# Output projections in pairs of column blocks with seven block products, in a two-layer decoder trunk

## The chip, the core and the metric

The kernel runs on one core of a Trainium2 chip. The core has a matrix engine (PE in the profile, with its weight loads listed as PEld), a vector engine (DVE), a scalar engine (ACT), a general engine (POOL) and SyncE (SP), which here only issues DMAs. Operands lie in SBUF, products are accumulated in eight PSUM banks of 128 x 512 float32. The metric is the device time of one launch in microseconds.

## What is computed

Two pre-norm layers on 256 tokens with 2048 columns, all in float32:

```
for layer in (0, 1):
    xn  = rms_norm(h, norm_mix[layer])
    mix = swa_mlstm_mixer(xn) if layer == 0 else forgetting_attention_mixer(xn)
          # each ends in:  concat(heads) @ w_out        (256 x 2048) @ (2048 x 2048)
    h   = h + mix
    h   = h + swiglu(rms_norm(h, norm_ffn[layer]))      # w_gate, w_up: 2048 x 5632, w_down: 5632 x 2048
out = rms_norm(h, norm_final)
```

The layer 0 mixer has sixteen heads of sliding-window attention (columns 0 to 1023 of its output) and four mLSTM heads (columns 1024 to 2047, 256 each). The layer 1 mixer has sixteen attention heads of 128 columns. The change concerns the product `concat(heads) @ w_out` of both layers.

## The kernel before

**Products.** A float32 product is made from three faster ones: each operand is split into a high part (rounded, a cast on ACT) and a low part (the rest, a subtraction on DVE), and hi x hi, lo x hi and hi x lo are summed in PSUM. Activations are kept split and transposed, in `xh`/`xl` (the normed stream) and `mh`/`ml` (the mixer's output, later the hidden values of the feed-forward part). Each has 16 k tiles of 128 rows by 256 tokens; two neighbouring k tiles are a pair, 0 to 7, and the tokens are two halves t of 128. Weights come in chunks of two k tiles by 512 columns (512 KB): `load_raw` (L101) issues the DMA on SP's queue, `split_chunk` (L156) casts on ACT (L159) and subtracts on DVE (L160). A chunk feeds 12 matmuls of 128 x 512.

**Seven products.** `pair_group` (L373) treats two column blocks at once and walks the eight pairs of k in a given order. A pair marked 0 is plain: two chunks, 24 matmuls. A pair marked 1 is mixed: its 2 x 2 x 2 block product (k tile by token half by column block) is done with 7 block products instead of 8, 21 matmuls. This needs sums of the two weight chunks `ra` and `rb` (tile `t4`, four DVE instructions, L404 to L407), the splits of them (`ht`, `lt`), the high and low parts of the last row of `rb` (`hu`, `lu`) and sums of the four activation blocks (`sums_of`, L222). Three of the seven products go into the plain accumulators, four into banks of their own:

```
three(prods[0], xa[:, t0], la[:, t0], hg[:, 0, :], lg[:, 0, :], first, last)
three(plain[0][0], xb[:, t0], lb[:, t0], hg[:, 1, :], lg[:, 1, :], False, False)
three(plain[1][0], sh[:, 3, :], sl[:, 3, :], hu[:, 1, :], lu[:, 1, :], False, False)
three(prods[1], sh[:, 0, :], sl[:, 0, :], ht[0], lt[0], first, last)
three(prods[2], sh[:, 2, :], sl[:, 2, :], ht[1], lt[1], first, last)
three(prods[3], sh[:, 1, :], sl[:, 1, :], ht[2], lt[2], first, last)
three(plain[0][1], xb[:, t1], lb[:, t1], ht[3], lt[3], False, False)
```

At the end of a group one ACT copy and four DVE additions (L430 to L434) make `c` from the four banks, and `c` is added to the result. Before the change the feed-forward part alone uses `pair_group`; gate and up have three mixed pairs of eight.

**PSUM.** Two pools of four banks: `pa` (tag `acc`) and `pm` (tag `pm`). `bank(par, name)` (L370) picks the pool: a group's four plain accumulators come from one pool and its four product banks from the other, alternating. Attention, mLSTM and all transposes use `pm`.

**SBUF.** `close_layer` (L548) opens the pool `fp` for output projection and feed-forward part together. The mixer's own pools (`ev` with `mp` in it for layer 0, `od` for layer 1) are closed by then in the program's text, so `fp` may be laid where they were. In `fp` are the weight chunks of mixed pairs (`raw`, four slots, `load_raw(..., fp)`), `t4`, `ht`, `lt`, `c`, and the activation sums `sx` and `sd`. Plain chunks use `wr` (four raw slots) and `wp` (six slots each of `hi` and `lo`), which are open all the time; `hg` and `hu` of a mixed pair use `wp` too.

**Order.** Each engine runs a fixed list of instructions. A planner makes it before the run: it walks through the program with its own estimate of durations and gives each engine the first instruction in program order whose operands and buffers it takes to be ready. So later work can be placed between instructions of earlier work.

**The output projection before.** `out_proj` (L353) takes column blocks two by two, n0 = 0 and 2 (called first and second half here). For both blocks it runs k tiles 0 to 11 (six pairs) with `gemm` (L173), then for one block after the other the last four k tiles (pairs 6 and 7), the residual addition `add_out` (L267), `split_scaled` (L233: transposes into `pt`, scaled splits into `xh`/`xl`, and `sums_of` for three pairs that the feed-forward part mixes) and `square_sum`. All four accumulators are in `pa`; `pt` is in `pm`.

**What comes ahead of it.** In layer 0: the V projections (L807) and, for each of four heads, `mlstm` (L768): `pc` (L770), its copy `ce` on DVE (L771), two products `pom` (L777, L779), a normalisation over DVE, ACT and POOL on `hv`, and the transposes `ptv` (L802) that become one pair of `mh`/`ml`: head 0 gives pair 4, head 3 pair 7. In layer 1: `attention` on four heads at a time; the last call gives pairs 6 and 7 (`po`, L341 and L342).

Of the kernel before, what the change touches and what calls it, by code (L numbers as in the profile page):

```python
# [7 lines left out]
F32 = mybir.dt.float32  # L8
# [4 lines left out]
ALU = mybir.AluOpType  # L13
# [4 lines left out]
P = 128  # L18
D = 2048
S = 256  # L20
NT = S // P
KT = D // P
FF = 5632
NB = 512
# [13 lines left out]
    6: ((0, 0), (0, 1), (1, 2), (0, 3), (0, 4), (0, 5)),  # L38
    8: ((0, 0), (0, 1), (0, 3), (1, 2), (0, 4), (1, 5), (0, 6), (0, 7)),
}  # L40
MID = 6
MID_DOWN = 5
RAWS = 4
# [3 lines left out]
def mixed_of(order):  # L47
    return [p for w, p in order if w]
# [5 lines left out]
def trunk(  # L54
# [20 lines left out]
    nc = tc.nc  # L75
# [89 lines left out]
    def new_acc():  # L165
        return [pa.tile([P, NB], F32, tag="acc", name="acc") for _ in range(NT)]
# [6 lines left out]
    def gemm(acc, lhs, w, c0, n, k_from, k_to, k_all, skew=1):  # L173
        k0 = k_from
        while k0 < k_to:
            last = k_to == k_all and k0 + skew * CK >= k_all
            chunks = [load_chunk(w, kc, c0, n) for kc in range(k0, k_all if last else k0 + CK, CK)]
            order = [(i, t) for i in range(len(chunks) * CK) for t in range(NT)]
            if last:
                order.sort(key=lambda it: it[1])  # L180
            for i, t in order:
                k = k0 + i
                hi, lo = (c[:, i % CK, 0:n] for c in chunks[i // CK])
                ah, al = lhs(k)
                ts = slice(t * P, (t + 1) * P)
                o = acc[t][:, 0:n]
                nc.tensor.matmul(o, ah[:, ts], hi, start=(k == 0), stop=False)  # L187
                nc.tensor.matmul(o, ah[:, ts], lo, start=False, stop=False)  # L188
                nc.tensor.matmul(o, al[:, ts], hi, start=False, stop=(k == k_all - 1))  # L189
            k0 += len(chunks) * CK  # L190
# [14 lines left out]
    def square_sum(key, n):  # L205
        if n == 0:
            sums[key] = sm.tile([P, NT, 4], F32, tag="ss", name="ss")
        for t in range(NT):
            junk = sm.tile([P, NB], BF16, tag="junk", name="junk", bufs=1)
            nc.scalar.activation(  # L210
                junk, h[:, t, n * NB : (n + 1) * NB], AF.Square, accum_out=sums[key][:, t, n : n + 1]
            )
# [17 lines left out]
        nc.vector.tensor_tensor(out=s[:, 3, :], in0=full[:, 1, 0, :], in1=s[:, 1, :], op=ALU.subtract)  # L230
        split_plain(sh, sl, s)

    def split_scaled(idx, n, extra=None):  # L233
        for half in range(2):
            pt = pm.tile([P, 2, NT, P], F32, tag="pm", name="pt")
            for i in range(2):
                k = 4 * n + 2 * half + i
                for t in range(NT):
                    nc.tensor.transpose(pt[:, i, t, :], h[:, t, k * P : (k + 1) * P], ident)  # L239
            for i in range(2):  # L240
                k = 4 * n + 2 * half + i
                src = pt[:, i, :, :].rearrange("p t q -> p (t q)")
                g = gT[:, idx * KT + k : idx * KT + k + 1]
                nc.scalar.mul(xh[:, k, :], src, g)
                nc.vector.scalar_tensor_tensor(
                    out=xl[:, k, :], in0=src, scalar=g, in1=xh[:, k, :].bitcast(F32), op0=ALU.mult, op1=ALU.subtract
                )
# [16 lines left out]
    def add_out(acc, n):  # L264
        for t in range(NT):
            o = h[:, t, n * NB : (n + 1) * NB]
            nc.vector.tensor_tensor(out=o, in0=acc[t], in1=o, op=ALU.add)  # L267
# [82 lines left out]
            ks = slice(k_tile + q, k_tile + q + 2)  # L350
            split_plain(mh[:, ks, :], ml[:, ks, :], po)

    def out_proj(w, idx, key, extra):  # L353
        last = KT - 4
        for n0 in (0, 2):
            accs = [new_acc() for _ in range(2)]
            for i in range(2):
                gemm(accs[i], m_of, w, (n0 + i) * NB, NB, 0, last, KT)
            for i in range(2):
                gemm(accs[i], m_of, w, (n0 + i) * NB, NB, last, KT, KT)  # L360
                add_out(accs[i], n0 + i)
                split_scaled(idx, n0 + i, extra)
                square_sum(key, n0 + i)

    def three(o, ah, al, hi, lo, start, stop):
        nc.tensor.matmul(o, ah, hi, start=start, stop=False)  # L366
        nc.tensor.matmul(o, ah, lo, start=False, stop=False)  # L367
        nc.tensor.matmul(o, al, hi, start=False, stop=stop)  # L368

    def bank(par, name):  # L370
        return pm.tile([P, NB], F32, tag="pm", name=name) if par else pa.tile([P, NB], F32, tag="acc", name=name)
# [65 lines left out]
    def ffn(layer, fp, sx, sd, key, idx_next=None, key_next=None, finish=None):  # L437
# [6 lines left out]
        for g0, g1 in zip(PARTS, PARTS[1:]):  # L444
# [82 lines left out]
            for n0 in (0, 2):  # L527
                if end and idx_next is None and n0 == 2:
                    for n in (2, 3):
                        acc = new_acc()  # L530
                        gemm(acc, m_of, wd, n * NB, NB, 0, nk, nk, skew=3 if n == 3 else 1)
                        close(acc, n)
                    continue
                plain, c = pair_group(
                    fp, 1 - n0 // 2, m_of, sums_d, [(wd, n0 * NB), (wd, (n0 + 1) * NB)], order, todo
                )
                todo = []
                if end and idx_next is None:
                    gf = fp.tile([P, D], F32, tag="t4", name="gf", bufs=1)
                    nc.gpsimd.dma_start(gf, norm_final.partition_broadcast(P))  # L540
                for m in range(2):
                    for t in range(NT):
                        o = h[:, t, (n0 + m) * NB : (n0 + m + 1) * NB]
                        nc.vector.tensor_tensor(out=o, in0=c[:, 2 * m + t, :], in1=o, op=ALU.add)
                for m in range(2):
                    close(plain[m], n0 + m)

    def close_layer(layer, w_out, idx, key, **rest):  # L548
        with tc.tile_pool(name=f"fp{layer}", bufs=2) as fp:
            nx = len(mixed_of(ORDER))  # L550
            nd = max(len(mixed_of(o)) for o in DOWN.values())
            sx = [fp.tile([P, nx, 4, P], F32R, name=f"sx{i}", bufs=1) for i in range(2)]
            sd = [fp.tile([P, nd, 4, P], F32R, name=f"sd{i}", bufs=1) for i in range(2)]
            out_proj(w_out, idx, key, (*sx, fp))
            ffn(layer, fp, sx, sd, key, **rest)


# [418 lines left out]
```

## Time and profile before

| | |
|---|---|
| launches | 2135.59, 2135.94, 2136.30 us (median 2135.94) |
| profiled execution | span 2134.3 us from the first to the last instruction |
| VectorE, ScalarE, GpSimd busy | 1665.9, 1235.5, 40.4 us |
| PE's waits of over 1 us in the whole span | 4.1 and 1.1 us for the first loads, 1.2 us for `mh` (L261) |
| HBM read | 404.48 MB, 191 GB/s over the span |

A row of the timeline has start and duration in us, engine, line, operation, output and inputs with their shapes, a count, and in brackets the idle time before it and what ended it. Matmuls are pipelined: a row's duration of 0.39 us overlaps the next, so the distance between starts is what a matmul costs. "SPq" is the queue of DMA issues; when several are merged, the duration reaches from the first to the last.

### The profile page before, as it was taken

How to read it: one execution, taken by the hardware profiler on the slowest of the kernel's cores; microseconds unless marked ns; L12 is line 12 of the kernel's file. 1: busy time of each engine (PE TensorE's matmuls, PEld its weight loads, DVE VectorE, ACT ScalarE, POOL GpSimd, SP SyncE). 2: the span in 40 equal slices, each digit the busy share in tenths (PEclk: the TensorE clock that was granted, in tenths of full speed). 3: DMA queues.
4: the chain of work that ended last, by engine and by line, in shares of the span. 5: the costliest groups of instructions: out<-in, count | busy, mean ns of one | idle time of the engine just before them, and what ended most of it. 6: DMA issues, size and time to landing. Idle time of an engine off the chain costs nothing.

```text
span 2134.3 us, 26801 instructions
## 1 busy us (share of the span) xinstructions
PE 2118.0 (99%) x9772; PEld 1758.6 (82%) x9772; DVE 1665.9 (78%) x2116; ACT 1235.5 (58%) x1564; POOL 40.4 (2%) x61
## 2 busy tenths in 40 slices
PE   8999999999999999999999999999999999999998
PEld 7888888888888888888888888888888888888886
DVE  6665567998899988998745554768998998889984
ACT  6565455665567646666645544556754667556753
POOL 2010000000000000000010000000000000000000
PEclk9999999999999999999999999999999999999999
DMA  8444556666667666776575564655756666656753
GB/s 268 149 151 145 174 183 206 214 210 194 200 205 223 212 206 193 236 210 191 152 236 168 168 178 141 234 185 174 246 187 215 207 207 199 234 188 207 227 198 128
DMA packets 257060, 418.84 MB, mean 196 GB/s; under 512 B 56256, under 2 KB 64544, under 8 KB 256672
## 3 DMA queue, kind: packets, MB, share of 16 engines
q1 hardware_dynamic: 256256, 413.40, 61.1%
q0 software_dynamic: 624, 3.72, 0.5%
q8 instruction: 76, 1.25, 0.2%
q14 instruction: 56, 0.46, 0.1%
q10 hardware_dynamic: 48, 0.02, 0.0%
HBM read 404.48 MB, written 2.11 MB: 191 GB/s over the span
## 4 chain that ended last, share of the span: by engine, by line
PE 98%; ACT 1%; issue 0%; DMA 0%; DVE 0%; POOLq 0%; POOL 0%; DVEq 0%; ACTq 0%
PE acc L367 17%; PE acc L368 17%; PE acc L366 17%; PE acc L187 10%; PE acc L188 10%; PE acc L189 10%; PE prod L368 4%; PE prod L367 4%; PE prod L366 4%; PE pt L239 1%; PE p L290 1%; PE ptm L273 1%; PE po L341 1%; PE pp L333 0%; PE p L283 0%
## 5 line engine op out<-in xcount | busy, mean ns | idle before, releaser
L159 ACT CAST hi<-raw 128x1024 fp32r<-128x1024 f32 (+1 forms) x692 | 705.7, 1033 | 681.2 <-PE acc L368 308.4
L160 DVE TENSOR_TENSOR lo<-raw,hi 128x1024 fp32r<-128x1024 f32 (+1 forms) x692 | 820.4, 1198 | 317.9 <-ACT hi L159 316.3
L367 PE MATMUL acc<-lo,xh 128*128 128x512 f32 x946 | 368.1, 389 | 0.0
L368 PE MATMUL acc<-hi,xl 128*128 128x512 f32 x946 | 366.8, 389 | 0.0
L366 PE MATMUL acc<-hi,xh 128*128 128x512 f32 x946 | 366.4, 389 | 0.0
L187 PE MATMUL acc<-hi,xh 128*128 128x512 f32 (+3 forms) x736 | 276.6, 377 | 0.8 <-ACT hi L159 0.8
L189 PE MATMUL acc<-hi,xl 128*128 128x512 f32 (+3 forms) x736 | 276.6, 376 | 0.0
L188 PE MATMUL acc<-lo,xh 128*128 128x512 f32 (+3 forms) x736 | 276.3, 375 | 0.0
L368 PEld LDWEIGHTS acc<-hi,xl 128*128 128x128 f32 x946 | 177.6, 188 | 36.8
L367 PEld LDWEIGHTS acc<-lo,xh 128*128 128x128 f32 x946 | 177.6, 188 | 36.8
L366 PEld LDWEIGHTS acc<-hi,xh 128*128 128x128 f32 x946 | 177.6, 188 | 36.8
L262 DVE TENSOR_TENSOR lt<-t,ht 128x1024 fp32r<-128x1024 f32 x168 | 199.6, 1216 | 3.6 <-ACT ht L261 3.6
L367 PE MATMUL acc<-lo,mh 128*128 128x512 f32 x514 | 200.3, 390 | 0.0
L366 PE MATMUL acc<-hi,mh 128*128 128x512 f32 x514 | 200.1, 389 | 0.0
L368 PE MATMUL acc<-hi,ml 128*128 128x512 f32 x514 | 198.6, 389 | 0.0
L261 ACT CAST ht<-t 128x1024 fp32r<-128x1024 f32 x168 | 175.0, 1053 | 23.2 <-PE acc L368 13.1
L187 PEld LDWEIGHTS acc<-hi,xh 128*128 128x128 f32 x736 | 138.8, 189 | 24.9 <-ACT hi L159 1.2
L189 PEld LDWEIGHTS acc<-hi,xl 128*128 128x128 f32 x736 | 139.1, 189 | 24.3 <-issue 0.8
L188 PEld LDWEIGHTS acc<-lo,xh 128*128 128x128 f32 x736 | 139.1, 189 | 24.1 <-issue 0.7
L187 PE MATMUL acc<-hi,mh 128*128 128x512 f32 x320 | 125.8, 393 | 1.2 <-ACT mh L261 1.2
L188 PE MATMUL acc<-lo,mh 128*128 128x512 f32 x320 | 125.7, 393 | 0.0
L189 PE MATMUL acc<-hi,ml 128*128 128x512 f32 x320 | 124.0, 390 | 0.0
(306 smaller groups left out, 2768.4 us busy)
## 6 DMA issues: line engine op xcount, KB each, us to landing
raw<-in_w_gate_dram SPq DMA_DIRECT2D x176, 512.0 KB, 4.1
raw<-in_w_up_dram SPq DMA_DIRECT2D x176, 512.0 KB, 4.5
raw<-in_w_down_dram SPq DMA_DIRECT2D x176, 512.0 KB, 4.6
raw<-in_w_in_odd_dram SPq DMA_DIRECT2D x88, 512.0 KB, 3.8
raw<-in_w_in_even_dram SPq DMA_DIRECT2D x64, 512.0 KB, 3.8
raw<-in_w_out_even_dram SPq DMA_DIRECT2D x32, 512.0 KB, 3.5
raw<-in_w_out_odd_dram SPq DMA_DIRECT2D x32, 512.0 KB, 3.9
raw<-in_w_in_odd_dram SPq DMA_DIRECT2D x8, 272.0 KB, 2.9
```

The lines of the kernel that those rows point to most:

```text
L159: latest[0] = nc.scalar.copy(hi[:, :, 0:n], raw[:, :, 0:n])
L160: nc.vector.tensor_tensor(out=lo[:, :, 0:n], in0=raw[:, :, 0:n], in1=hi[:, :, 0:n].bitcast(F32), op=ALU.subtract)
L187: nc.tensor.matmul(o, ah[:, ts], hi, start=(k == 0), stop=False)
L188: nc.tensor.matmul(o, ah[:, ts], lo, start=False, stop=False)
L189: nc.tensor.matmul(o, al[:, ts], hi, start=False, stop=(k == k_all - 1))
L239: nc.tensor.transpose(pt[:, i, t, :], h[:, t, k * P : (k + 1) * P], ident)
L261: nc.scalar.copy(dst_h, src)
L262: nc.vector.tensor_tensor(out=dst_l, in0=src, in1=dst_h.bitcast(F32), op=ALU.subtract)
L273: nc.tensor.transpose(pt[:, i, :], s_, ident)
L366: nc.tensor.matmul(o, ah, hi, start=start, stop=False)
L367: nc.tensor.matmul(o, ah, lo, start=False, stop=False)
L368: nc.tensor.matmul(o, al, hi, start=False, stop=stop)
```

## The change

Both output projections now go through `pair_group`, a half at a time. Pairs 0 and 1 of k are mixed and the other six plain; `OUT` gives the order for each half: the first half begins with plain pairs 2, 3, 4 and takes mixed pairs 0 and 1 at the fourth and the sixth place, the second half takes them at the second and the fifth. The sums of the activations are made at the beginning from `mh + ml`, into `sd` of the pool `fp`. The first half has its accumulators in `pa` and its products in `pm`, the second half the other way round; `split_scaled` takes `pt` from the pool of the half's accumulators. `add_pair` is the addition of `c` to the residual stream, moved out of the feed-forward part.

```diff
+OUT = (
+    ((0, 2), (0, 3), (0, 4), (1, 0), (0, 5), (1, 1), (0, 6), (0, 7)),
+    ((0, 2), (1, 0), (0, 3), (0, 4), (1, 1), (0, 5), (0, 6), (0, 7)),
+)
...
-    def split_scaled(idx, n, extra=None):
+    def split_scaled(idx, n, extra=None, par=1):
         for half in range(2):
-            pt = pm.tile([P, 2, NT, P], F32, tag="pm", name="pt")
+            pt = bank(par, "pt").rearrange("p (i t q) -> p i t q", i=2, t=NT)
...
-    def out_proj(w, idx, key, extra):
-        last = KT - 4
-        for n0 in (0, 2):
-            accs = [new_acc() for _ in range(2)]
-            for i in range(2):
-                gemm(accs[i], m_of, w, (n0 + i) * NB, NB, 0, last, KT)
-            for i in range(2):
-                gemm(accs[i], m_of, w, (n0 + i) * NB, NB, last, KT, KT)
-                add_out(accs[i], n0 + i)
-                split_scaled(idx, n0 + i, extra)
-                square_sum(key, n0 + i)
+    def out_proj(w, idx, key, extra, fp, sd):
+        mixed = mixed_of(OUT[0])
+        for j, pair in enumerate(mixed):
+            full = fp.tile([P, 2, NT, P], F32, tag="tmp", name="full")
+            ks = slice(2 * pair, 2 * pair + 2)
+            nc.vector.tensor_tensor(
+                out=full.rearrange("p i t q -> p i (t q)"),
+                in0=mh[:, ks, :].bitcast(F32),
+                in1=ml[:, ks, :].bitcast(F32),
+                op=ALU.add,
+            )
+            sums_of(fp, sd[0][:, j, :, :], sd[1][:, j, :, :], None, full)
...
+        for half in range(2):
+            n0 = 2 * half
+            plain, c = pair_group(fp, half, m_of, sums_m, [(w, n0 * NB), (w, (n0 + 1) * NB)], OUT[half])
+            add_pair(c, n0)
+            for m in range(2):
+                add_out(plain[m], n0 + m)
+                split_scaled(idx, n0 + m, extra, half)
+                square_sum(key, n0 + m)
...
+    def add_pair(c, n0):
+        for m in range(2):
+            for t in range(NT):
+                o = h[:, t, (n0 + m) * NB : (n0 + m + 1) * NB]
+                nc.vector.tensor_tensor(out=o, in0=c[:, 2 * m + t, :], in1=o, op=ALU.add)
...
-            out_proj(w_out, idx, key, (*sx, fp))
+            out_proj(w_out, idx, key, (*sx, fp), fp, sd)
```

More of the change, by code (lines that the diff above doesn't have):

```diff
@@ L351, in attention, with sums_m @@
             split_plain(mh[:, ks, :], ml[:, ks, :], po)
-    def out_proj(w, idx, key, extra):
-        last = KT - 4
-        for n0 in (0, 2):
-            accs = [new_acc() for _ in range(2)]
-            for i in range(2):
-                gemm(accs[i], m_of, w, (n0 + i) * NB, NB, 0, last, KT)
-            for i in range(2):
-                gemm(accs[i], m_of, w, (n0 + i) * NB, NB, last, KT, KT)
-                add_out(accs[i], n0 + i)
-                split_scaled(idx, n0 + i, extra)
-                square_sum(key, n0 + i)
+    def out_proj(w, idx, key, extra, fp, sd):
[10 more added lines that the diff above has]
+            sums_of(fp, sd[0][:, j, :, :], sd[1][:, j, :, :], None, full)
+        def sums_m(pair):
+            j = mixed.index(pair)
+            return sd[0][:, j, :, :], sd[1][:, j, :, :]
+        for half in range(2):
[11 more added lines that the diff above has]
+                nc.vector.tensor_tensor(out=o, in0=c[:, 2 * m + t, :], in1=o, op=ALU.add)
     def three(o, ah, al, hi, lo, start, stop):
@@ L540, in ffn @@
                     nc.gpsimd.dma_start(gf, norm_final.partition_broadcast(P))
[L541 to L544, printed above, removed]
+                add_pair(c, n0)
                 for m in range(2):
```

## The prediction

> **What bounds the kernel now.** I read the page first: busy shares and the chain that ended last.
>
> ```profile
> PE 2118.0 (99%) x9772; PEld 1758.6 (82%) x9772; DVE 1665.9 (78%) x2116; ACT 1235.5 (58%) x1564; POOL 40.4 (2%) x61
> PE 98%; ACT 1%; issue 0%; DMA 0%; DVE 0%; POOLq 0%; POOL 0%; DVEq 0%; ACTq 0%
> ```
>
> The matrix engine is never without work for long, and the chain is 98% PE: a matmul taken away shortens the kernel, and a hole opened in PE's row lengthens it. So I looked at what PE does around the output projections. First the cost of a matmul and the beginning of the first half in layer 0 (timeline of PE), then how many of its matmuls were done when (stretches of PE restricted to `mh`; hi x hi and lo x hi read `mh`, so 2 of 3 matmuls count, 128 for the 192 of a half).
>
> ```profile
> 253.43 0.39 PE L187 MATMUL acc<-hi,mh 128*128 128x512 f32 x1
> ...
> 254.11 0.39 PE L187 MATMUL acc<-hi,mh 128*128 128x512 f32 x1
> ...
> 253.43:298.19 44.76, 36.03 (x113) 20.85 (x112) 1.36 (x2) 1.74 (x3) 1.00 0.48 166
> 253.43:303.79 50.36, 40.61 (x128) 23.77 (x127) 2.04 (x3) 1.74 (x3) 1.00 0.54 184
> 1338.99:1386.05 47.06, 39.34 (x126) 23.64 (x126) 1.38 (x2) 1.17 (x2) 1.00 0.69 228
> ```
>
> A matmul costs 0.227 us (0.68 for three). In layer 0 the half runs from 253.43 to 303.79, in layer 1 from 1338.99 to 1386.05. At 298.19 some 168 of the 192 were done (113 x 1.5): all but pair 7. That work is the cover under which the mixer's tail runs:
>
> ```profile
> 264.99 0.60 PE L802 MATMUL ptv<-ident,hv 128*128 128x128 f32 x4
> 265.43 0.60 PE L770 MATMUL pc<-ve,kw 128*128 128x257 f32 x2
> 265.86 1.03 PE L777 MATMUL pom<-ve,dt__1258 128*128 128x257 f32 x4
> 266.06 0.42 DVE L771 COPY ce<-pc 128x257 f32<-128x257 f32 x1 [1.51 <-PE pc L770]
> 270.84 0.59 PE L779 MATMUL pom<-ce,qst 128*128 128x257 f32 x2
> 274.77 0.89 DVE L791 SCALAR_TENSOR_TENSOR hv<-hv,st,og 128x256 f32<-128x256 f32 x2 [1.22 <-POOL st L789]
> 279.45 0.60 PE L802 MATMUL ptv<-ident,hv 128*128 128x128 f32 x4
> 296.41 0.60 PE L802 MATMUL ptv<-ident,hv 128*128 128x128 f32 x4
> 298.19 0.50 PE L187 MATMUL acc<-hi,mh 128*128 128x512 f32 x1 [1.18 <-ACT mh L261]
> ```
>
> The mLSTM heads follow each other at 15 to 17 us (the three `ptv` rows). A head's `pc` has its inputs long before, yet starts right behind the transposes of the head ahead (264.99 and 265.43): the buffers of one tag, here `pm`, are handed out in program order. While a head waits, PE does output projection, so that its whole tail of 44.8 us costs PE one hole of 1.18 us.
>
> The last view is SP's queue around the end of each mixer, with SP's waits in the same stretches. The feed-forward part's first mixed pairs are prefetched here: four loads into `raw` of `fp`.
>
> ```profile
> 227.94 68.65 SPq L103 DMA_DIRECT2D raw<-in_w_out_even_dram  x23
> 297.08 0.37 SPq L103 DMA_DIRECT2D raw<-in_w_gate_dram  x1
> 297.50 0.46 SPq L103 DMA_DIRECT2D raw<-in_w_up_dram  x1
> SPq L103 <- PE ptv L802: 0.4, 1, 0.4
> 1360.41 0.38 PE L342 MATMUL po<-t,vtail 128*128 128x128 f32 x2
> 1360.87 0.37 SPq L103 DMA_DIRECT2D raw<-in_w_gate_dram  x1
> 1361.29 0.46 SPq L103 DMA_DIRECT2D raw<-in_w_up_dram  x1
> SPq L103 <- PE po L342: 0.9, 1, 0.9
> ```
>
> In both layers the loads go out right after the mixer's last read of its own tiles (the transposes of `hv`, the last `po`), and SP waits for just these. A load into `fp` has no other tie to `ptv` or `po`: `fp` lies where the mixer's pools lay and opens only when they are done. Before the change nothing in `fp` is needed for 50 us after that.
>
> **The change part by part.** *Removed*: two pairs of eight in each of four halves take 21 matmuls instead of 24: 4 x 2 x 3 = 24 matmuls x 0.227 = 5.4 us, all on the bounding engine; 1.36 us per half.
>
> *Moved, first half*: the mixed pairs' weights, their sums and splits, and the sums of the activations all lie in `fp`, so none can be made before the mixer ends. What PE has ahead of the first mixed pair is three plain pairs, 72 matmuls = 16.3 us, in place of 168. May pair 5 go ahead of the mixed pair? Its `hi` and `lo` come behind `hg` and `hu` in the tag's order, and by the `pc` rows such an order is kept; I take no. The product banks are in `pm` behind `ptv` or `po` in the same way, which comes free at the same time as `fp` and costs nothing more. Loads on SP behind the waiting ones are for pairs which cannot run anyway.
>
> Layer 0: PE does 49 of the 72 by 264.99 (11.56 us less about 0.4 for head 1's L779) and runs dry at about 272.4 (23 x 0.227 behind `pc` and `pom`, which end at 266.7). From there the heads do not wait for PE's fillers: head 2's `hv` is ready at 275.66 (274.77 + 0.89), while its transposes now start at 279.45; then head 3 needs from its first `pom` to `hv` what head 2 needed, 265.86 to 275.66 = 9.8 us, less about 3.5 us by which L779 (270.84, behind fillers) lagged the end of `ce` (266.48). That puts the end of `ptv` at about 283.7, against 297.0 if nothing is shortened; I take 284, since with no filler there is nothing to wait behind. Then the loads. The first pair of `fp` loads landed as follows (the DVE's first use, ended by the DMA):
>
> ```profile
> 304.60 0.69 DVE L404 TENSOR_TENSOR t<-raw 128x512 f32<-128x512 f32 x1 [2.65 <-DMA raw<-in_w_up_dram]
> 1367.80 0.69 DVE L404 TENSOR_TENSOR t<-raw 128x512 f32<-128x512 f32 x1 [3.05 <-DMA raw<-in_w_up_dram]
> raw<-in_w_out_even_dram SPq DMA_DIRECT2D x14, 512.0 KB, 3.5
> ```
>
> That is 7.1 us (from 297.50) and 6.5 us (from 1361.29), with other loads in flight; alone a chunk takes 3.5. Bounds 3.5 and 7.1 us; I take 6, since four chunks go together. So landing at about 290. Then a mixed pair's preparation, from the groups by shape (the ACT row from the page):
>
> ```profile
> L160 DVE TENSOR_TENSOR lo<-raw,hi 128x1024 fp32r<-128x1024 f32 x660 | 797.7, 1221 | 298.0 <-ACT hi L159 296.6
> L159 ACT CAST hi<-raw 128x1024 fp32r<-128x1024 f32 (+1 forms) x692 | 705.7, 1033 | 681.2 <-PE acc L368 308.4
> L262 DVE TENSOR_TENSOR lt<-t,ht 128x1024 fp32r<-128x1024 f32 x168 | 199.6, 1216 | 3.6 <-ACT ht L261 3.6
> L404 DVE TENSOR_TENSOR t<-raw 128x512 f32<-128x512 f32 x84 | 57.5, 685 | 6.8 <-DMA raw<-in_w_up_dram 5.7
> L262 DVE TENSOR_TENSOR lo<-raw,hi 128x512 fp32r<-128x512 f32 x84 | 57.7, 686 | 28.2 <-ACT hi L261 27.7
> L267 DVE TENSOR_TENSOR h<-acc,h 128x512 f32<-128x512 f32 x56 | 37.4, 680 | 3.1 <-PE acc L189 1.8 <-PE acc L368 1.3
> L245 DVE SCALAR_TENSOR_TENSOR xl<-pt,gT,xh 128x256 fp32r<-128x256 f32 x64 | 28.4, 477 | 9.0 <-ACT xh L244 8.7
> ```
>
> On DVE 1.22 + 4 x 0.685 + 0.69 + 2 x 1.22 = 7.1 us, against 4.8 us of PE (21 matmuls) and against 2.4 us of DVE for a plain pair. Of the 186 matmuls 114 are left: 25.8 us on PE, plus 1.0 for the first cast and about 1.2 more because PE catches up with DVE in the first mixed pair: 28 us after landing, 318. Before, the same point was 303.8: **+14 us**.
>
> Layer 1: its half took 47.06 us for 43.5 us of matmuls, so 3.5 us of PE went to attention, about half of it ahead of `po`: 72 matmuls from 1338.99 end at 1357; `po` may move up by half a microsecond, the pool opens at about 1360.2, landing 1366.3, end 1394.3, against 1386.05: **+8 us**.
>
> *Added, hidden*: `full` and the sums of two activation pairs on DVE, at most 2 x (0.69 + 4 x 0.48 + 0.69) = 6.6 us (the 128-column additions priced as the 256-column row), run while the loads are in flight; without that cover they would delay the first mixed pair by as much. The `c` of each half (one ACT copy and four additions of 0.68) and `add_pair` (four of 0.68) come while PE does pairs 6 and 7, 48 matmuls = 10.9 us.
>
> *Second halves*: no gate there. DVE per half: 12 x 1.22 + 2 x 7.1 + 12 x 0.68 + 8 x 0.48 + 2.6 for one pair of feed-forward sums = 43 us, for 186 matmuls (42.2) and 16 transposes (1.8) = 44 us of PE. It just fits, with the first mixed pair at the second place, just behind the boundary where DVE also has `add_out`, the splits and the sums. The product banks there (`acc`) come behind four `pt`. Bounds 0 to 3 us of hole for each, none seen at the feed-forward groups' boundaries, whose first mixed pair is a place later; I take 0.5. So -1.36 + 0.5, twice: **-1.7 us**.
>
> *Clock.* PE's first work after idling runs at half speed. The chain of waits near the start:
>
> ```profile
> 9.47 1.81 PE pt L239 x8
> 11.28 0.43 PE acc L188
> 14.04 0.87 PE pt L239 x8
> 15.37 0.23 PE acc L188
> ```
>
> Eight transposes take 1.81 us and later 0.87, a matmul 0.43 and later 0.23; from 8.25 to 12.14 this cost some 2.1 us. Behind a hole of 7 to 17 us the same may come back, but in those microseconds PE would be waiting for DVE's 7.1 us anyway: 12 matmuls at 0.43 are 5.2 us. I add nothing; the bounds are 0 and 2.1 us for each of two holes. The Trainium skill ("TensorE: Matmul & The Clock Gate", Part 1: The HAM clock gate) states such a gate: after a window of about 3.4 us without activity the array runs at half rate until it has been busy for as long. The duration rows at the start agree in kind, though the granted clock reads 1.00 there. By that page the changed kernel would start cold in both layers, an estimated 1.7 us each if nothing hid it; this would speak for the upper half of the range.
>
> **Sum**: 14 + 8 - 1.7 = +20.3 us on a span of 2134.3. The launches' median is 2135.94, 1.64 above the span, so 2156.2.
>
> **The rivals.**
> *Plain pairs run ahead.* If the buffers of `hi` and `lo` need not go in order, pairs 5 and 6 fill PE in layer 0 (120 matmuls, dry at about 286), the heads are then not shortened by much (`ptv` ends at 293, landing 299), and the two preparations of 14 us decide: end at 315, +11. In layer 1 pairs 5 to 7 cover nearly everything: 186 x 0.227 + 3.5 = 45.7 us against 47.1, of which I give half to DVE's catching up: -0.6. With -1.7: +9, 2145. For it: PE does take matmuls of one accumulator out of order when one is blocked. Against: the `pc` rows.
>
> *The heads are not shortened.* If the planner's list keeps the tail as long as now, `fp` opens at 297.0, landing 303, end 331 (+27); layer 1 +9; -1.7: +34, 2170. For it: the list is made from estimates, and ACT and DVE have new work to put between. Against: no filler is left for PE.
>
> *Faster.* If the first mixed pair's loads could go out early enough, by about 265 in layer 0 (so that 7 us later PE is just running dry) and 1350 in layer 1, nothing is uncovered, and the 24 matmuls come off: 2135.9 - 5.4 = 2130.5. That needs `fp` to be laid over tiles that are dead by then (queries, keys), tile by tile instead of as a whole. For it: no row shows which addresses overlap. Against: the loads of both layers went out together, right at the last read of the mixer, and SP's waits name just that.
>
> **How the numbers follow.** Forecast 2156, chance 0.5; plain pairs ahead 2145, 0.2; heads not shortened 2170, 0.18; faster 0.09; holes and savings that cancel 0.03. The range 2140 to 2174 takes in the first three with their bounds for landing (-2.5, +1 per layer), clock and second halves, and leaves out the faster case and the far ends of the others. A difference under 0.2% (4 us) can't be told from no change. Faster 0.09, same 0.03, slower 0.88.
>
> **What would show it.** Right: two `raw<-in_w_out_even_dram` loads first in `fp`'s order right behind the last `ptv`; a hole in PE, broken only by mLSTM matmuls, ended by ACT's `hi` or DVE's `lt`; `ptv` of head 3 earlier than 296; a smaller hole around 1357 to 1367; no holes over 3 us in the second halves; 24 matmuls fewer. Wrong: `fp` loads of `w_out` issued before the mixer's last read, or matmuls of pair 5 ahead of the first `prod`, or new holes in the feed-forward part.

## The result and the profile after

| | before | after |
|---|---|---|
| median of the launches | 2135.99 us | 2153.18 us (2151.96 to 2153.99, 4 runs) |
| profiled execution, span | 2134.3 us | 2152.3 us |
| ratio | | 1.0081, 95% interval 1.0067 to 1.0096 |
| matmul instructions, PE | 9772 | 9748 (24 fewer) |
| VectorE busy | 1665.9 us | 1721.3 us |

The kernel got 17.2 us slower; the forecast was 20. The page of the changed kernel, busy shares and the chain that ended last:

```profile
PE 2120.2 (99%) x9748; PEld 1757.4 (82%) x9748; DVE 1721.3 (80%) x2220; ACT 1250.1 (58%) x1588; POOL 40.2 (2%) x61
...
PE 94%; DVE 3%; ACT 1%; issue 1%; DMA 1%; POOL 0%; POOLq 0%; ACTq 0%; DVEq 0%; SPq 0%
```

PE's busy time did not fall with the 24 matmuls, and 4% of the chain went over from PE to DVE, ACT and DMA. DVE's 3% lie mostly in two stretches, 348 to 377 us and 1434 to 1467, where the output projection ends and the feed-forward part begins: the chain runs through DVE there, although PE waits for only 0.5 and 0.2 us. DVE has no time to spare at these places, which matters below. PE's waits over the whole span, in columns total, times and longest:

```profile
PE prod L389 <- ACT hi L163: 11.0, 2, 5.6
PE ptv L822 <- DVE hv L811: 5.2, 2, 4.0
```

One wait in each layer, of 5.6 and 5.4 us, for the first cast of a mixed pair, and in layer 0 two waits for the heads. PE's timeline in layer 0 shows both (start, duration; idle time before in brackets):

```profile
272.81 0.39 PE L391 MATMUL acc<-hi,ml 128*128 128x512 f32 x1
274.45 0.33 PE L822 MATMUL ptv<-ident,hv 128*128 128x128 f32 x1 [1.25 <-DVE hv L811]
...
280.82 1.30 PE L822 MATMUL ptv<-ident,hv 128*128 128x128 f32 x4 [3.98 <-DVE hv L811]
287.71 0.79 PE L389 MATMUL prod<-hi,mh 128*128 128x512 f32 x1 [5.59 <-ACT hi L163]
...
290.06 0.63 PE L390 MATMUL acc<-lo,mh 128*128 128x512 f32 x1
290.49 0.63 PE L391 MATMUL acc<-hi,ml 128*128 128x512 f32 x1
...
294.49 0.39 PE L390 MATMUL acc<-lo,mh 128*128 128x512 f32 x1
294.72 0.40 PE L391 MATMUL acc<-hi,ml 128*128 128x512 f32 x1
```

The 72 plain matmuls are done at 273.0 and from there PE has only the heads. After the hole matmuls start 0.43 us apart until about 293, then 0.23: half speed. What PE waits for is on SP and ACT. SP's waits in the stretch from 225 to 330, then the timeline of SP's issues and of ACT:

```profile
SPq L107 <- PE ptv L822: 24.5, 1, 24.5
```

```profile
282.27 11.93 SPq L107 DMA_DIRECT2D raw<-in_w_out_even_dram  x7
...
286.61 1.04 ACT L163 CAST hi<-raw 128x1024 fp32r<-128x1024 f32 x1 [1.53 <-DMA raw<-in_w_out_even_dram]
```

SP stood 24.5 us at the first load into `fp` until the last `ptv` was done. The load was issued at 282.27, the data was there at 286.61, and the cast took 1.04 us. Layer 1 has the second hole alone; PE does plain pairs right up to the last `po`:

```profile
1368.58 0.40 PE L391 MATMUL acc<-hi,ml 128*128 128x512 f32 x1
1368.81 0.60 PE L345 MATMUL po<-t,vn 128*128 128x256 f32 x2
...
1371.21 0.38 PE L346 MATMUL po<-t,vtail 128*128 128x128 f32 x2
1377.02 0.80 PE L389 MATMUL prod<-hi,mh 128*128 128x512 f32 x1 [5.43 <-ACT hi L163]
```

To share the loss between the layers I compare points that both programs pass in the same order: `pf`, the transposes at the end of each feed-forward part's first half, and `pp`, an early attention step of layer 1. From the chain of waits, first before, then after:

```profile
491.82 0.66 PE pf L471 x6
...
1352.73 0.66 PE pp L333 x6
...
1574.75 0.66 PE pf L471 x6
```

```profile
504.48 0.66 PE pf L494 x6
...
1364.67 0.66 PE pp L337 x6
...
1593.71 0.66 PE pf L494 x6
```

The changed program is 0.6 us late already at 171 us, 12.7 late after layer 0's output projection, 11.9 late when layer 1 begins its own, and 19.0 late after it (18.0 at the end). So layer 0's projection lost some 12 us and layer 1's some 7, of which about 1 is given back in each feed-forward part; I count **+11.3 and +6.1 us net**.

### The profile page after: what moved, and what is told of

Read it like the earlier page. It is cut to its first block, busy times and chain, and to the rows that moved or that the text cites. A ratio compares the mean times of both kernels' runs of the same rounds, so it can differ in the third digit from the quotient of the medians.

```text
span 2152.3 us, 26882 instructions
## 1 busy us (share of the span) xinstructions
PE 2120.2 (99%) x9748; PEld 1757.4 (82%) x9748; DVE 1721.3 (80%) x2220; ACT 1250.1 (58%) x1588; POOL 40.2 (2%) x61
## 3 DMA queue, kind: packets, MB, share of 16 engines
q8 instruction: 76, 1.25, 0.2%
## 4 chain that ended last, share of the span: by engine, by line
PE 94%; DVE 3%; ACT 1%; issue 1%; DMA 1%; POOL 0%; POOLq 0%; ACTq 0%; DVEq 0%; SPq 0%
PE acc L391 19%; PE acc L389 19%; PE acc L390 19%; PE acc L191 8%; PE acc L193 8%; PE acc L192 8%; PE prod L389 4%; PE prod L391 4%; PE prod L390 4%; DVE lo L164 1%; PE p L294 1%; PE ptm L277 1%; PE po L345 1%; PE pt L243 0%; PE pp L337 0%
## 5 line engine op out<-in xcount | busy, mean ns | idle before, releaser
L163 ACT CAST hi<-raw 128x1024 fp32r<-128x1024 f32 (+2 forms) x684 | 697.6, 1033 | 644.0 <-PE acc L391 330.1
L164 DVE TENSOR_TENSOR lo<-raw,hi 128x1024 fp32r<-128x1024 f32 (+2 forms) x684 | 813.1, 1201 | 277.5 <-ACT hi L163 276.3
L390 PE MATMUL acc<-lo,mh 128*128 128x512 f32 x714 | 279.2, 391 | 0.0
L391 PE MATMUL acc<-hi,ml 128*128 128x512 f32 x714 | 277.4, 391 | 0.0
L389 PE MATMUL acc<-hi,mh 128*128 128x512 f32 x714 | 276.4, 392 | 0.0
L266 DVE TENSOR_TENSOR lt<-t,ht 128x1024 fp32r<-128x1024 f32 x184 | 220.1, 1221 | 4.1 <-ACT ht L265 4.0
L265 ACT CAST ht<-t 128x1024 fp32r<-128x1024 f32 x184 | 191.0, 1052 | 41.5 <-PE prod L391 12.4
L389 PEld LDWEIGHTS acc<-hi,mh 128*128 128x128 f32 x714 | 135.2, 189 | 28.2
L390 PEld LDWEIGHTS acc<-lo,mh 128*128 128x128 f32 x714 | 134.3, 188 | 28.0
L391 PEld LDWEIGHTS acc<-hi,ml 128*128 128x128 f32 x714 | 134.3, 188 | 27.8
```

The lines of the kernel that those rows point to most:

```text
L163: latest[0] = nc.scalar.copy(hi[:, :, 0:n], raw[:, :, 0:n])
L164: nc.vector.tensor_tensor(out=lo[:, :, 0:n], in0=raw[:, :, 0:n], in1=hi[:, :, 0:n].bitcast(F32), op=ALU.subtract)
L265: nc.scalar.copy(dst_h, src)
L266: nc.vector.tensor_tensor(out=dst_l, in0=src, in1=dst_h.bitcast(F32), op=ALU.subtract)
```

## The experiments

My theory: the time is set by a *gate*. The pool `fp` opens at the mixer's last read, and the first half cannot take its mixed pairs before, so PE's cover runs out. The main rival is *DVE*: a mixed pair costs DVE 7.1 us, and it might be DVE that PE follows, gate or not. Each run has the kernel before beside it (2135.6 to 2136.0 us).

**One half alone.** The second half only (the first half is the old code):

```diff
+            if half == 0:
+                accs = [new_acc() for _ in range(2)]
+                for i in range(2):
+                    gemm(accs[i], m_of, w, (n0 + i) * NB, NB, 0, KT - 4, KT)
...
+                continue
             plain, c = pair_group(fp, half, ...)
```

> First half of both output projections as before the change (plain, accumulated by gemm), second half in mixed pairs. Gate theory (the loss is made where the first mixed pair has to wait for the mixer's last read, in the first halves alone): 12 matmuls fewer, no hole over 1 us behind the mixers, second halves 1.36 us shorter each less up to 0.5 us: 2133 to 2135 us, a little faster than before. DVE theory (the loss is the added DVE work of mixed pairs, which is as large in the second halves): about half of the 17 us stays, 2144 us.

Measured 2142.83 us, ratio 1.0036 (1.0023 to 1.0048). PE's timeline in layer 0, then a window (length; busy time of PE, PEld, DVE, ACT, POOL; granted clock, DMA share, GB/s):

```profile
304.92 0.87 PE L243 MATMUL pt<-ident,h 128*128 128x128 f32 x6 [1.52 <-DVE h L271]
...
307.10 0.79 PE L399 MATMUL prod<-ht,sd 128*128 128x512 f32 x1 [1.30 <-ACT ht L265]
...
311.12 0.50 PE L400 MATMUL prod<-lt,sd 128*128 128x512 f32 x1 [1.10 <-DVE lt L266]
```

```profile
300.00:320.00 20.00, 14.55 (x56) 10.64 (x55) 19.07 (x35) 14.59 (x27) 0.00 (x0) 0.83 0.51 178
```

Here the mixed pair at the second place is wanted at 302 to 304, `fp` has been open since 296.4, and now waits of 1.1 to 1.5 us stand on `h`, `ht` and `lt`: on DVE, which is busy for 19.07 of 20 us, and on casts of what DVE made. The gate has a hand in it: DVE's first `t` waited for its load until 302.97, 6.6 us after `fp` opened. Layer 0 lost some 6 us and layer 1, where the same half comes later after `po`, won half a microsecond. Nearer to the DVE theory: a second half has its own loss, which in the whole change is covered, since there the first half ends 9 us after what it did before and DVE has had that time.

The first half only (the second is the old code), once with `pt` of the first half in `acc` as in the change, once with `pt` in `pm` (the last two lines of the diff):

```diff
+            if half == 1:
+                accs = [new_acc() for _ in range(2)]
...
+                continue
...
-                split_scaled(idx, n0 + m, extra, half)
+                split_scaled(idx, n0 + m, extra)
```

> The opposite: first half in mixed pairs, second half as before the change. Gate theory: the holes of the changed kernel at the same places, and 12 matmuls more than there: 2153.2 + 2 = 2155 us. DVE theory: 2144 us.

> First half in mixed pairs, second half as before the change, and the first half's transposes pt in pm, so that the second half's accumulators in acc do not stand behind them. Gate theory: the changed kernel plus what its second halves save, 2153 + 2 = 2155 us. If the 50 us of the first such run came from mixed pairs and not from pt ahead of the accumulators: 2170 us or more.

Measured 2185.89 us (1.0235, 1.0219 to 1.0251) and 2165.87 us (1.0142, 1.0127 to 1.0158): both worse than the whole change, and no theory had said so. PE's waits of the first:

```profile
PE pt L243 <- DVE h L271: 15.1, 3, 8.0
PE prod L399 <- ACT hi L163: 10.8, 2, 5.5
```

The gate's two holes are there unchanged (10.8 us). The 15.1 us are the run's own: with `pt` and the old second half's accumulators both in `acc`, the second half stands behind `pt`, and `pt` behind `add_out`. With `pt` in `pm` that goes, but in each layer some 3 us for `lo` come, in layer 0 between 321 and 325; DVE is busy for 19.50 of the 20 us from 320 on. A half alone is thus no clean piece of the change: which pool of banks the next half takes belongs to it. That DVE causes these 3 us I read from its window; it was not tried.

**How much plain work goes ahead.** All plain pairs but one ahead of the mixed ones in the first half (cover of 120 matmuls), or only one (24); the two added lines are the two orders:

```diff
-    ((0, 2), (0, 3), (0, 4), (1, 0), (0, 5), (1, 1), (0, 6), (0, 7)),
+    ((0, 2), (0, 3), (0, 4), (0, 5), (0, 6), (1, 0), (1, 1), (0, 7)),
+    ((0, 2), (1, 0), (0, 3), (0, 4), (1, 1), (0, 5), (0, 6), (0, 7)),
```

> The changed kernel with the first half's mixed pairs at the sixth and seventh place, behind plain pairs 2 to 6, ahead of pair 7. Same instructions, other order. Gate theory: the cover grows from 72 to 120 matmuls (27.2 us); layer 1 needs no hole, layer 0 is dry at about 286 and starts again at about 294: 2138 to 2142 us. DVE theory: the same work is done, only closer together: 2150 us or more.

> The changed kernel with the first half's mixed pairs at the second and fifth place, as in the second half. Same instructions, other order. Gate theory: the cover shrinks from 72 to 24 matmuls; the mLSTM heads gain part of the 10.9 us by running without fillers, so some +8 us in layer 0 and +7 in layer 1 over the changed kernel: 2165 to 2170 us. DVE theory: no change, 2153 us.

Measured 2149.8 us (1.0066, 1.0052 to 1.008) and 2159.91 us (1.0114, 1.01 to 1.0127). Late cost little less than the change, early little more. The timelines of PE, late and early:

```profile
286.57 0.60 PE L822 MATMUL ptv<-ident,hv 128*128 128x128 f32 x4
...
292.40 0.80 PE L389 MATMUL prod<-hi,mh 128*128 128x512 f32 x1 [5.23 <-ACT hi L163]
...
301.60 0.50 PE L389 MATMUL acc<-hi,sd 128*128 128x512 f32 x1 [0.98 <-ACT sd L265]
...
311.44 0.73 PE L389 MATMUL prod<-ht,sd 128*128 128x512 f32 x2 [1.44 <-ACT ht L265]
```

```profile
274.69 1.30 PE L822 MATMUL ptv<-ident,hv 128*128 128x128 f32 x4 [4.52 <-DVE hv L811]
...
281.16 0.80 PE L389 MATMUL prod<-hi,mh 128*128 128x512 f32 x1 [5.17 <-ACT hi L163]
```

With 24, 72, 120 and (before) 168 matmuls ahead, the last `ptv` starts at 274.69, 280.82, 286.57 and 296.41: 48 matmuls (10.9 us) more move the gate back by 6 to 10 us, because the heads' steps stand behind PE's filler work. And from the end of `ptv` to the first product there are 5.17, 5.59 and 5.23 us, whatever is ahead. The gate theory without the moving gate had said some 13 us for each order; both lie within 7 us of the change.

The moving gate explains the early order: 10.9 us of cover less, but the first product 6.6 us earlier, and layer 0 is 3.2 us later at `pf`. It does not explain the late one. There the first product comes 4.7 us later with 10.9 us more work behind it, a gain of 6.2 us, and still `pf` is as late as with the change (504.29 against 504.48). The gain goes into new waits behind the gate, for `ht`, `sd`, `lt`, `hi` and `xh`: 5.0 us in all up to 378, where the change has 0.5. With what PE loses around each wait, its gaps beyond 0.23 us from the first product to 378 come to 9.6 us, against 3.7. From 300 to 320 DVE is busy for 18.78 of 20 us:

```profile
300.00:320.00 20.00, 16.47 (x68) 12.08 (x67) 18.78 (x24) 10.43 (x14) 0.00 (x0) 1.00 0.64 213
```

The chain that ended last runs mostly through DVE from 292 to 316. So with less plain work left beside it, the preparation sets the pace in layer 0, as the DVE theory has it (it had said 2150 us or more). In layer 1, where `po` does not wait for fillers, late was worth 3.7 us (+2.4 instead of +6.1 net): the hole of 5.4 us is gone, but 3.4 us of small waits for `sd`, `ht` and `lo` stand in its place. The late order also has both mixed pairs next to each other.

**The load out of the gate.** The raw chunks of the first half's mixed pairs come from `wr`, which is open all the time:

```diff
-            plain, c = pair_group(fp, half, m_of, sums_m, [...], OUT[half])
+            plain, c = pair_group(fp, half, m_of, sums_m, [...], OUT[half], raws=wr if half == 0 else None)
...
-            ra, rb = (load_raw(w, k0, c0, NB, fp) for w, c0 in mats)
+            ra, rb = (load_raw(w, k0, c0, NB, fp if raws is None else raws) for w, c0 in mats)
```

> The changed kernel with the raw chunks of the first half's mixed pairs in the pool wr, which is open all the time; sums, splits and t4 stay in fp. If the hole behind the mixer is the wait for loads that cannot go out earlier: the hole ended by the cast hi (5.4 us in each layer) goes, pair 5 runs ahead of it, and PE stays warm in layer 1; what is left is the preparation on DVE: 2141 to 2148 us. If it is the preparation on DVE anyway: 2152 us or more.

Measured 2150.8 us (1.0069, 1.0056 to 1.0083), between the two expectations. PE's waits in layer 0, 250 to 330, and the restart in its timeline:

```profile
PE acc L389 <- ACT ht L265: 7.2, 1, 7.2
PE ptv L822 <- DVE hv L811: 4.0, 1, 4.0
```

```profile
293.74 0.80 PE L389 MATMUL acc<-ht,mh 128*128 128x512 f32 x1 [7.21 <-ACT ht L265]
```

The wait for the load is gone and a longer one has taken its place: for `ht`. `t4`, `ht` and `lt` are in `fp` too, so this part of the preparation still starts at the gate. The gate itself opens later as well: the planner put six first products (283.33 to 286.03) between the first and the other three transposes of the last head. So layer 0 gained nothing (`pf` at 504.78). In layer 1 the hole shrank from 5.4 to 2.7 us, and that layer became 3.7 us shorter. What the gate holds is the whole preparation, and taking out one piece of it does little where the rest of it is just as late.

**Clock and DVE in the first half.** First, twelve unread matmuls behind the last `ptv` and `po`, to keep PE at full rate while it waits:

```diff
+        idle = pm.tile([P, NB], F32, tag="pm", name="idle")
+        side = mh[:, 14:16, :].rearrange("p k s -> p (k s)")
+        for i in range(12):
+            nc.tensor.matmul(idle, mh[:, 14, 0:P], side, start=(i == 0), stop=(i == 11))
```

> The changed kernel with 12 matmuls of 128x512 into a bank of pm that nobody reads, in the hole behind the mixer's last read (they read the last pair of mh). They do not take part in the result. If the half speed after the hole costs its 2.8 us in each layer on the path: 5 us less, 2148 us. If those microseconds are hidden behind the preparation on DVE: 2153 us.

Measured 2153.7 us (1.0084, 1.007 to 1.0098), the same as the change. Its timeline:

```profile
281.17 5.49 PE L377 MATMUL idle<-mh 128*128 128x512 f32 x12 [0.68 <-ACT mh L265]
286.45 0.63 PE L393 MATMUL prod<-hi,mh 128*128 128x512 f32 x1
...
288.27 0.50 PE L393 MATMUL acc<-hi,sd 128*128 128x512 f32 x1 [0.78 <-ACT hi L265]
...
290.17 0.50 PE L393 MATMUL acc<-hi,mh 128*128 128x512 f32 x1 [0.25 <-ACT hi L163]
...
292.06 0.73 PE L393 MATMUL prod<-ht,sd 128*128 128x512 f32 x2 [0.45 <-ACT ht L265]
```

From 288.6 on the products start 0.23 us apart, but three waits for casts follow. With what PE loses before and after each, the gaps beyond 0.23 us add up to some 2.7 us from 286.4 to 292.6, and the half-speed matmuls of the change cost 2.6 us (12 of them, about 0.2 each, the first 0.36). One takes the place of the other.

Then DVE's `lt` taken out of the output projections' mixed pairs, alone and together with the unread matmuls (these kernels leave out a part of the sum and take `ht` twice, with as many matmuls):

```diff
-                split_plain(hs, ls, t4[:, 2 * i : 2 * i + 2, :])
+                if bare:
+                    nc.scalar.copy(hs, t4[:, 2 * i : 2 * i + 2, :])
+                    ls = hs
+                else:
...
```

> The changed kernel without the lo half of the weight combinations in the output projections' mixed pairs (the subtraction `lt` is left out, the products take `ht` twice; as many matmuls as with the change): 2 x 1.22 = 2.4 us of DVE less for each mixed pair, 4.9 us per half. Theory A (behind the gate DVE's preparation sets the pace on its own, PE merely follows): each first half ends 2 to 4 us sooner, together 2145 to 2149. Theory B (the gate's hole and PE's slow matmuls behind it just cover DVE's preparation, so that either alone changes nothing): PE was busy from the restart at 287.7 on and stays so; 2152 to 2153.5.

> The same cut together with the 12 unread matmuls that keep PE at full rate in the hole (as in the run with those alone, which took 2153.7). Theory B: with both covers gone the first products run at 0.227 us and no DVE work holds them: 2 to 3 us less per first half, 2147 to 2149. Theory A: the same as without the unread matmuls, within 1 us. If the loads alone set the end (a third theory): 2153 in both.

Measured 2151.06 us (1.0073, 1.0059 to 1.0087) and 2150.63 us (1.0069, 1.0053 to 1.0084). 9.8 us less of DVE work per layer bring 2.1 us in all (3.1 between the profiled executions), so in the order of the change DVE is not what sets the first half's end: theory A, which had said 2145 to 2149, falls. But both covers gone together bring no more either, so B, as I had put it, falls too. The timeline without `lt`:

```profile
279.88 0.94 PE L826 MATMUL ptv<-ident,hv 128*128 128x128 f32 x4 [3.98 <-DVE hv L815]
...
286.01 0.79 PE L389 MATMUL prod<-hi,mh 128*128 128x512 f32 x1 [5.19 <-ACT hi L163]
```

`ptv` ends 1.3 us earlier than with the change, in the planner's new order, and the products follow it by 5.19 us: they restart 1.7 us earlier, which is more than half of the 3.0 us by which layer 0's `pf` is earlier (501.47 against 504.48), and owes nothing to the preparation behind the gate. In layer 1 there are 0.3 us. What stands behind the half speed is, by the waits, the string of casts (`hi` of three chunks, `hu`, `ht`), which waits for loads as they land and is untouched by this cut. No run took these casts away, so this is read from the waits and not shown.

**The second half later.** Second half only, with the mixed pairs at the fourth and sixth place, accumulators and `pt` in the pools of the old code:

```diff
-            plain, c = pair_group(fp, half, m_of, sums_m, [...], OUT[half])
+            plain, c = pair_group(fp, 0, m_of, sums_m, [...], OUT[0])
...
-                split_scaled(idx, n0 + m, extra, half)
+                split_scaled(idx, n0 + m, extra)
```

> First half as before the change, second half in mixed pairs at the fourth and sixth place instead of the second and fifth, its accumulators in the pool acc and its products in pm behind the transposes pt. Gate theory as it stands after the first four runs (what counts is how much plain work lies between the opening of fp and the first mixed pair): fp opens at 297 as before, the first mixed pair comes at 320, loads and preparation take 13 us, so no hole is left and 12 matmuls come off: 2133 to 2135 us, faster than before. If the second halves cost by DVE work whatever the place: 2140 us or more, as in the run with the second half at the second place (2142.8).

Measured 2139.41 us (2136.53 to 2140.84 in 11 runs; 1.0014, 1.0005 to 1.0023): still slower than before, where the gate theory had said faster. Then the same without `lt`, and the same in full with `t4` on GpSimd (the other three subtractions likewise):

```diff
-            nc.vector.tensor_tensor(out=t4[:, 0, :], in0=rb[:, 0, :], in1=ra[:, 0, :], op=ALU.subtract)
+            (eng or nc.vector).tensor_tensor(out=t4[:, 0, :], in0=rb[:, 0, :], in1=ra[:, 0, :], op=ALU.subtract)
...
```

> First half as before, second half mixed at places 4 and 6 (2139.4 with the whole work), without `lt` in it: 4.9 us of DVE less in each second half. If DVE's load is what takes back the 12 matmuls there: layer 0 loses 3 to 5 us of its hole, 2134 to 2135.5. If the gate or the banks do: 2138.5 to 2139.5.

> The same with the whole computation, the four subtractions `t4` of a mixed pair on GpSimd instead of DVE (2.7 us of DVE less per pair, 5.5 per half; GpSimd's nearest row of 512 columns took 1.29 us, so some 5.2 us a pair in a row there). If DVE's load decides and GpSimd costs DVE nothing: 2134.5 to 2136, the first version that is not slower than before. If GpSimd's longer chain or a slower DVE beside it decides: 2139 or more.

Measured 2134.29 us (0.9993, 0.9984 to 1.0002) and 2137.8 us (1.0009, 1.0 to 1.0017). Windows of layer 0, in the columns of the windows above, with the whole work, and PE's hole there:

```profile
320.00:340.00 20.00, 20.00 (x90) 16.57 (x89) 19.11 (x28) 12.75 (x19) 0.00 (x0) 1.00 0.69 229
340.00:360.00 20.00, 17.33 (x68) 13.49 (x67) 19.17 (x31) 10.71 (x19) 0.69 (x1) 0.83 0.46 146
```

```profile
353.26 0.79 PE L400 MATMUL acc<-lo,xh 128*128 128x512 f32 x1 [2.08 <-DVE lo L164]
```

The same windows without `lt`:

```profile
320.00:340.00 20.00, 20.00 (x90) 16.53 (x90) 18.27 (x28) 14.66 (x19) 0.00 (x0) 1.00 0.74 240
340.00:360.00 20.00, 19.28 (x93) 15.75 (x92) 18.63 (x31) 10.77 (x23) 0.69 (x1) 1.00 0.53 160
```

With the whole work DVE is busy for 38.3 of 40 us, and PE pays with 68 matmuls in a window that has room for some 90. The hole stands at the first products of the feed-forward part, on a `lo` that DVE made late, and not on `lt` itself: it is the load on DVE that counts. With 4.9 us less of DVE work per half the hole shrinks to 0.7 us, the low clock goes, and the median falls by 5.1 us (the profiled executions by 6.4, 5.8 of it in layer 0, `pf` at 490.54 after 496.34). A part of this is the clock: of the 11 launches with the whole work, seven with a mean granted clock of 0.996 took 2139.3 to 2140.8 us, and four with 0.998 or 0.999 took 2136.5 to 2138.2. So in a second half whose first mixed pair is wanted soon after the gate, DVE's load is the limit.

With `t4` on GpSimd the time lies between the two expectations, and its launches (2136.1 to 2139.47 us) overlap those with `t4` on DVE. DVE in layer 0, in its groups by shape from 296 to 325:

```profile
L164 DVE TENSOR_TENSOR lo<-raw,hi 128x1024 fp32r<-128x1024 f32 x8 | 12.5, 1557 | 1.2 <-ACT hi L163 1.2
...
L249 DVE SCALAR_TENSOR_TENSOR xl<-pt,gT,xh 128x256 fp32r<-128x256 f32 x8 | 3.5, 471 | 0.0
```

`lo` takes 1557 ns on the mean against 1214 with `t4` on DVE. With `lt`, `sd` and the sums, DVE's instructions in these rows took some 6 us longer, so the 5.5 us that left DVE came back as longer instructions. No version here was faster than before by a measurable amount.

Taken together: with the first half left as it was, the loss falls from 17.2 us to 7.3 and 3.4, so most of it is made in the first halves, where the pool opens late and PE runs out of work. What a longer cover or an earlier load would then gain is in layer 0 used up by the preparation behind the gate; in layer 1 each of the two brought 3.7 us.

## Why the prediction was right, step by step

*The gate.* Right in each part: the loads into `fp` went out just behind the last `ptv` (282.27) and `po` (1371.72), pair 5 did not go ahead of the first product, and PE was dry at 273.0 (forecast 272.4). The heads were shortened: `ptv` ended at 282.1, forecast 284 against 297 unshortened. Part of the difference is in the forecast's own rows: L779 lagged the end of `ce` by 4.4 us (270.84 less 266.48), where about 3.5 was taken; head 3 now needed 5.7 us from its first `pom` to `hv`, for the 6.3 of the sum. The early and late orders show that this step is a slope: cover and gate move together. Hence the rival in which the heads keep their length falls, and so does the one with plain pairs ahead. The late order is close to that rival's picture (120 matmuls in front) and took 2149.8, where I had put 2145; the waits for the preparation in layer 0 are what that rival left out.

*Landing.* Mis-sized: 6 us was taken, the first chunk was usable 4.3 us after its issue (282.27 to 286.61). The bounds came from the first `t`, which reads two chunks, while the first product needs one alone; the four chunks took 4.3 to 7.1 us, 5.8 in the median. This and the earlier `ptv` make the restart 287.7 instead of some 291.

*From landing to the half's end.* 28 us was taken. 26.3 passed from 286.6 to the first `pt` at 312.88, which is not quite the same, since the planner had by then put in some matmuls of the second half. By the points that both programs pass, layer 0 came to +11.3, where 14 less half of 1.7 is 13.2, and layer 1 to +6.1, where it is 7.2. In layer 0 it adds up in PE's row: holes of 1.25, 3.98 and 5.59 us, 0.7 for the slow last `ptv` (1.30 instead of 0.60), 2.6 for the half speed, less the 1.2 us hole of before and 2.7 for 12 matmuls: +10.2. Another 0.5 is a wait for `xl` further on. At `pf`, up to which this row goes, layer 0's projection is 12.1 us late, so some 1.4 I did not find. The sum's 1.2 us for PE catching up with DVE in the first mixed pair did not come as a wait; the 2.6 us of half speed, put at nothing, stand in the same place. That the total came within some 3 us of the forecast is thus partly luck: the landing and the heads were put too long, the restart too cheap.

*Layer 1.* The size was near, one detail was wrong: PE was not dry at 1357 (1368.9 in the time of the changed program) before `po` but busy up to it, so that its hole is the 5.4 us from `po` on alone.

*Clock.* That half speed would come and add nothing held: 12 matmuls ran at half rate in layer 0, and the run that kept PE warm gained nothing. But the cover that I named, DVE's 7.1 us, is only part of it; the waits that came up were for ACT's casts and for loads landing one after the other, and DVE's share of it is at most the 2 us that the cut of `lt` gave. By the Trainium skill ("TensorE: Matmul & The Clock Gate", Part 1: The HAM clock gate) PE is back at full rate after some 3.4 us of work; here it took 5.3 us in layer 0 (287.7 to 293.0) and 5.0 in layer 1 (1377.0 to 1382.0), which is longer, and in this the trace does not agree.

*Second halves.* In the changed kernel no hole was seen and the step held there. But as I read the runs with the second half alone, it held for a reason that I had not given: in layer 0 it starts late enough for DVE to be ready. With a first half that is not delayed, the same second half lost 6 us in layer 0 (at places two and five) or 5 (at four and six), and for the later places the cut of DVE's load shows why. My sum of 43 us of DVE against 44 of PE "just fits" left out that so little slack is gone when the first mixed pair is wanted soon after the pool opens.

*Faster.* Falls: SP's wait names `ptv` and `po`, as the row of before did.

## What to carry to other kernels

Before moving work ahead, ask from which instant on its buffers exist: a pool that takes over the place of another opens at the last read there, and all that is prepared in it, not the load alone, lies behind that instant. Work on the bounding engine that serves as cover for a chain can also slow the chain: here 10.9 us of cover more moved the restart back by 4.7 to 6.6 us. And a saving on the bounding engine that costs a second engine three times as much (7.1 us for 2.4) counts only where that second engine has the time in the same window; a mean of 78% busy does not tell it.

## What the hardware showed unexpectedly

GpSimd and DVE slowed each other in the run with `t4` on GpSimd. POOL's timeline and DVE's in the same stretch:

```profile
306.62 1.33 POOL L438 TENSOR_TENSOR t<-raw 128x512 f32<-128x512 f32 x1
307.91 2.28 POOL L439 TENSOR_TENSOR t<-raw,t 128x512 f32<-128x512 f32 x1
```

```profile
304.29 1.22 DVE L164 TENSOR_TENSOR lo<-raw,hi 128x1024 fp32r<-128x1024 f32 x1
...
306.74 2.30 DVE L164 TENSOR_TENSOR lo<-raw,hi 128x1024 fp32r<-128x1024 f32 x1
309.08 2.20 DVE L266 TENSOR_TENSOR lt<-t,ht 128x1024 fp32r<-128x1024 f32 x1
```

A subtraction on GpSimd takes 1.3 us or 2.2, a `lo` or `lt` on DVE 1.22 or 2.2 to 2.3. By the rows the two take turns: the subtraction ends at 307.95, the `lo` beside it at 309.04, the next subtraction at 310.19 and the `lt` at 311.28, each 1.1 to 1.2 us after the one before it. `xl`, which reads one operand from PSUM, kept its 471 ns; four of them ran from 317.15 to 318.80 beside subtractions, one of which took its short 1.30 us. The Trainium skill ("SBUF — State Buffer", Who interferes with whom) says that a DVE instruction with two SBUF inputs contends with a GpSimd instruction that reads SBUF, and one with at most one such input does not; the rows agree with both.

A short hole was enough for the low clock. In the run with the second half later, the matmul behind the wait of 2.1 us (353.26) was 0.60 us from the next, as behind the change's holes (0.59 at 287.71), and after another wait of 0.6 us matmuls stood 0.43 us apart from 356.8 to 359.8; the granted clock is 0.83 in the window from 340. In the second run with the first half alone a wait of 3.1 us at 321 to 325 was followed by a distance of 0.34 and then 0.23. So the length of the hole does not decide alone; what else does, no run here shows.
